# A hybrid mixer block on one core: new order of the products, gate projections between the mixers, VectorE in place of GpSimd

## The chip, the cores and the metric

The kernel runs on one core of a Trainium2 chip. The metric is the device time of one execution in microseconds (us), as the median over repeated executions. A core has five engines that work side by side: TensorE (PE in the profile, with its weight loads as PEld), VectorE (DVE), ScalarE (ACT), GpSimd (POOL) and SyncE (SP, which here only issues transfers). Each engine works through its own list of instructions in order, and waits on semaphores for the others.

## The reference, cut to what matters

One decoder layer on 512 tokens of width 1024, in float32: three token mixers of four heads each beside one another, merged by gates, and then an MLP.

```python
u = rmsnorm(x, g_norm_mix)
proj = u @ w_in                                   # q, k, v, gates of all three mixers
h_m = head_rmsnorm(sigmoid(mo) * mlstm(mq, mk, mv, li, lf), g_hm)
lg  = log_sigmoid(llr @ w_gla_lr + b_gla) / 16
h_l = head_rmsnorm(gla(lq, lk, lv, lg), g_hl) * silu(lr)
qkv = silu(causal_conv([dq, dk, dv], conv_w))     # then l2-normed per head
h_d = head_rmsnorm(gated_deltanet(gq, gk, gv, g_dec, beta), g_hd) * silu(dz)
up  = einsum('bsnc,ncd->bsnd', [h_m, h_l, h_d], w_up)
x   = x + sum_n(sigmoid(gates_n) * up_n) @ w_out
u   = rmsnorm(x, g_norm_mlp)
x   = x + square(relu(u @ w_mlp_in)) @ w_mlp_out
out = rmsnorm(x, g_final)
```

`mlstm`, `gla` and `gated_deltanet` are chunked recurrences along the sequence; the last solves a unit triangular system in each chunk.

## The kernel before, in words

Every large product (projections, up, out, MLP) is done in three passes: each operand is split into a rounded part (`h`) and the rest (`l`), and `mm3` (line 548) issues `al·bh`, `ah·bl`, `ah·bh` into one PSUM bank, 512 columns each. There are 3768 such passes, called wide products below: 96 each for `mv`, `mo`, `dz`, `lv` and `lr`, 24 for `sc`, 48 for each of the 14 projections `dk0` to `lk1` and the 12 gate groups `gt00` to `gt23`, 24 for each of the 12 `up` groups, 192 for `wo`, 768 each for the MLP's `mi` and `mo`. A weight tile of 128 x 1024 is loaded by SP's queue (`load_w`, line 622), rounded by ACT, and its rest is taken by DVE; it feeds 24 wide products. Between them stand small products in plain float32: transposes, and the mixers' 128 x 128 blocks and smaller.

The program is not issued as it is written. `write_block` (line 509) records operations into a graph, and a list scheduler in Python (`Graph.schedule`, line 232, and `run`, line 284) gives each a start time from a table of costs (`cost`, line 192) and emits them in that order on each engine. The wide products are "mains": their order is fixed by the list in `plan` (line 480). All else is placed around them, the operation with the earliest due time first; due times come from a backward pass over the graph. Tiles come from pools of fixed size: `s` has 55 buffers of 516 columns for nearly everything of 128 x 512, `raw`, `wh`, `wl` have three each for weights, `g` and `m` four PSUM banks each. When a pool is empty, an operation that needs a new tile of it stands later in the order.

The order of the mains before is: `mv mo sc`, the six projections of the delta branch (`dk dq dv`), the four of the mLSTM (`mq mk`), `dz`, then gates and up products of the mLSTM branch (`gt00 up00 gt01 up01 ...`), then `lv lq lk` for GLA, gates and up products of the delta branch (`gt20 up20 ...`), `lr`, those of the GLA branch (`gt10 up10 ...`), `wo`, and the MLP. `up0x` needs `hmT`, `up2x` needs `hdT`, `up1x` needs `hlT`, the finished outputs of the mixers.

The parts that the change touches:

- `gen_u` (line 594): eight squares of x on ACT, summed by seven POOL adds into `xacc`, while the first products (`mv`) run on x times the norm's gain.
- `conv_evac` (line 821): three DVE passes per head for the convolution, then a sigmoid on ACT and a product on POOL.
- `gen_scalars` (line 753), `gen_k` (837), `gen_q` (871): masks `em` (eight `s` tiles; two transfers, a POOL add, an exp each), and `ub`, the 32 x 32 diagonal blocks with their sign turned, by 32 small passes, half on POOL.
- `gen_gdn` (line 904): `ub` goes through DRAM into a layout `Z` in which a backward substitution runs as 60 dependent POOL passes (lines 914 to 918); its result `xb` comes back through DRAM, is copied into `em` by 32 small passes, and two levels of block inversion on PE follow, then the loop over four chunks.
- `gen_gla` (line 1134): per head a softplus, cumulative sums (four scans), and for seven block sizes L one or two POOL subtractions into `lw`, an exp on ACT, two DVE products (`lwq`, `lw`), PE products `ll` and copies into `lAT`.
- `merge` (1245), `gen_x2` (1303), `square_of` and `finish` (1398, 1405): more POOL adds and products on 128 x 512 tiles.

Of the kernel before, what the change touches and what calls it, by code (L numbers as in the profile page):

```python
# [12 lines left out]
ALU = mybir.AluOpType  # L13
# [10 lines left out]
SLOTN = 516  # L24
NWARM = 10
NSLOT = 55
# [22 lines left out]
INORDER = ("w", "mq")  # L49
RESERVE = {"s": 6, "m": 1}  # L50

# [54 lines left out]
class Op:  # L106
    __slots__ = ("i", "eng", "calls", "cost", "lat", "preds", "succs", "tiles", "main", "fset", "kind", "start", "fin", "lst", "npred", "ready", "new", "tag", "nbytes", "evac")


class Graph:  # L110
    def __init__(self, nc):
        self.nc = nc
        self.ops = []
        self.main_key = None
        self.open = None
        self.shadow = __import__("concourse.bacc", fromlist=["Bacc"]).Bacc("TRN2", target_bir_lowering=False, num_devices=1)
        self.ntile = 0
        self.gate = []
        self.tensor, self.vector, self.scalar, self.gpsimd, self.sync = (Eng(self, e) for e in ("tensor", "vector", "scalar", "gpsimd", "sync"))

# [30 lines left out]
    def record(self, eng, method, a, k):  # L151
# [7 lines left out]
        if fresh:  # L159
# [3 lines left out]
            op.tag = ""  # L163
            self.ops.append(op)
# [6 lines left out]
        c, lat = self.cost(eng, method, a, k, op)  # L171
# [20 lines left out]
    def cost(self, eng, method, a, k, op):  # L192
# [10 lines left out]
        if eng == "tensor":  # L203
            if method == "transpose":
                return max(0.109, n / 1200), 0.2
            if a[1].t.dt == F32R:
                return max(0.109, n / 2400 + 0.0135), 0.2
            return 2 * max(a[1].shape[-1] / 1200, n / 1200, 0.012) + 0.007, 0.2
        if eng == "scalar":
# [3 lines left out]
            c = 0.09 + n * 0.86e-3  # L213
            if any(isinstance(k.get(x), View) for x in ("bias", "scale")) or (method == "mul" and isinstance(a[2], View)):
                c += 0.08
            if k.get("accum_out") is not None:
                c += 0.11
            return c, 0.12
        if eng == "vector":
            if method in ("tensor_scalar", "tensor_scalar_mul", "tensor_copy", "tensor_scalar_add", "tensor_single_scalar", "memset", "reciprocal") and not ps:  # L220
                return 0.1 + n * (0.55e-3 if method != "reciprocal" else 1.05e-3), 0.1
            if method == "tensor_tensor_scan":
                return 0.12 + n * 2.1e-3, 0.1
            if method == "copy_predicated":
                return 0.1 + n * 1.3e-3, 0.1
            return 0.1 + n * 1.06e-3 + (0.05 if ps else 0), 0.1
        if method in ("memset", "tensor_copy"):
            return 0.15 + n * 0.8e-3, 0.1
        return 0.2 + n * 2.15e-3, 0.1


    def schedule(self, caps, seq, horizon, rounds=2, verbose=False):
# [12 lines left out]
        for r in range(rounds):  # L245
            for o in reversed(ops):
                l = end + 5 - o.cost
                for s in o.succs:
                    l = min(l, s.lst - self.edge(o, s) - o.cost)
                o.evac = o.eng != "tensor" and any(t.whole for t in o.tiles)  # L250
                if o.evac:
                    l = min([l] + [pin[p] + p.cost + EVAC for p in o.preds if p in pin])
                o.lst = min(l, pin[o]) if o in pin else l
            for o in ops:
                if o.evac:
                    o.lst = min(o.lst, max(p.lst + p.cost for p in o.preds) + EVAC)
# [15 lines left out]
        return sorted(ops, key=lambda o: (o.start, o.i))  # L272

# [10 lines left out]
    def run(self, mains, caps, horizon, verbose=False):  # L284
# [10 lines left out]
        waiting = {}  # L295
        for o in ops:
# [8 lines left out]
            if not o.npred and o.main is None:  # L305
                cand[o.eng].append(o)
# [5 lines left out]
        line = {c: [t for o in reversed(ops) for t in o.new if t.cls == c] for c in INORDER}  # L312
        urgent = {c: sorted((o for o in ops if any(t.cls == c for t in o.new)), key=lambda o: -o.lst) for c in RESERVE}
# [25 lines left out]
        while done < total:  # L339
# [4 lines left out]
            for e, fr in free.items():  # L344
# [39 lines left out]
                if bests is None or pick[2] < bests[0]:  # L384
                    bests = pick[2:]
# [15 lines left out]
            for w in waiting.pop(o, ()):  # L401
                w.npred -= 1
                w.ready = max(w.ready, T)
                if w.npred == 0 and w.main is None:
                    cand[w.eng].append(w)
            tight = True
            c = o.cost
# [26 lines left out]
            for s in o.succs:  # L434
# [5 lines left out]
                if s.npred == 0 and s.main is None:  # L440
                    cand[s.eng].append(s)
            if o.main is None:
                cand[o.eng].remove(o)
# [5 lines left out]
    def emit(self, order, pools, phys):  # L449
        nc = self.nc  # L450
        for o in order:
# [15 lines left out]
            for eng, method, a, k in o.calls:  # L467
                f = lambda x: x.real() if isinstance(x, View) else x
                getattr(getattr(nc, eng), method)(*[f(x) for x in a], **{n: f(x) for n, x in k.items()})  # L469
# [10 lines left out]
def plan():  # L480

    merge_of = lambda n: [x for dp in range(4) for x in (f"gt{n}{dp}", f"up{n}{dp}")]
# [1029 lines left out]
```

## Time and profile before

| | |
|---|---|
| median of 3 runs | 1022.69 us (1020.7 to 1024.67) |
| the profiled execution's own time | 1020.38 us |
| its span, first to last instruction | 1018.4 us |
| PE busy | 979.8 us, 96% (4992 products) |
| PEld, DVE, ACT, POOL busy | 809.1, 581.3, 404.7, 201.9 us |
| mean granted TensorE clock | 0.986 |

In the profile nearly every instruction has line L469, where `emit` issues it, so groups are told apart by their tiles. The span is cut into stretches in the second group of rows below. A stretch in which PE has all its time is one in which no mixer holds the products up; the number in brackets behind a busy time is the number of instructions. Because products are pipelined, a PE row lasts longer (0.39 us) than the distance to the next row's start (0.23 us), and a slow stretch can look busy: the distance between starts is the better measure.

### The profile page before, as it was taken

Reading aid. Unit: us, or ns where it says so; the run is one execution under the profiler, and the core shown is the slowest. Engines: PE = TensorE matmul, PEld = TensorE weight load, DVE = VectorE, ACT = ScalarE, POOL = GpSimd, SP = SyncE. Lnnn points to the kernel's source line nnn. Section 1 sums busy time; section 2 is a strip of 40 time slices with the busy share of each in tenths; the row PEclk is TensorE's granted clock in tenths of the full one; section 3 lists DMA queues with packets and bytes.
Section 4 is the critical chain, followed back from the end, with each engine's and each line's share of the span. In section 5 each row is a group of like instructions: output and inputs, shape, how many; then the busy total and the mean of one; then the engine's idle time right before and its main releaser. Section 6 shows DMA issues by size and latency. Waiting matters only on the chain.

```text
span 1018.4 us, 12973 instructions
## 1 busy us (share of the span) xinstructions
PE 979.8 (96%) x4992; PEld 809.1 (79%) x4992; DVE 581.3 (57%) x962; ACT 404.7 (40%) x748; POOL 201.9 (20%) x240
## 2 busy tenths in 40 slices
PE   7999999999996999889999999999999999999996
PEld 5888888787885888777888888888888888888885
DVE  7646634878733365999836454444444544544445
ACT  6342423877221546744324334443223232422412
POOL 4100100309593000867411002200000000100004
PEclk9999999999997999979999999999999999999999
DMA  6233232331423112211341223222333233432302
GB/s 237 83 104 96 90 104 96 102 105 53 113 74 84 63 63 91 63 62 43 104 145 63 91 95 104 83 83 83 107 101 104 73 113 97 138 117 83 104 21 83
DMA packets 37029, 94.65 MB, mean 93 GB/s; under 512 B 7804, under 2 KB 11900, under 8 KB 36968
## 3 DMA queue, kind: packets, MB, share of 16 engines
q1 hardware_dynamic: 36152, 92.51, 28.5%
q10 hardware_dynamic: 720, 1.08, 0.3%
q8 instruction: 39, 0.64, 0.3%
q0 software_dynamic: 96, 0.24, 0.1%
q14 instruction: 22, 0.18, 0.1%
HBM read 91.17 MB, written 2.65 MB: 92 GB/s over the span
## 4 chain that ended last, share of the span: by engine, by line
PE 83%; DVE 10%; issue 3%; ACT 3%; POOL 0%; DMA 0%; DVEq 0%; POOLq 0%; ACTq 0%
PE mop L469 19%; PE mip L469 17%; PE upp L469 5%; PE wop L469 4%; PE mvp L469 3%; PE lvp L469 2%; PE lrp L469 2%; DVE lw L469 1%; PE gt23p L469 1%; PE gt10p L469 1%; PE lk0p L469 1%; PE gt01p L469 1%; PE lq0p L469 1%; PE gt11p L469 1%; PE gt13p L469 1%
## 5 line engine op out<-in xcount | busy, mean ns | idle before, releaser
L469 DVE SCALAR_TENSOR_TENSOR x<-mop,r2c,x 128x512 f32<-128x512 f32 (+1 forms) x65 | 48.1, 740 | 61.0 <-PE mop L469 60.5
L469 POOL TENSOR_SCALAR gf<-gf 128x512 f32<-128x512 f32 x2 | 3.0, 1492 | 225.3 <-DMA gf<-in_g_fin_dram 225.3
L469 POOL TENSOR_TENSOR lw<-lbs 128x260 f32<-128x260 f32 (+12 forms) x52 | 42.6, 846 | 17.3 <-PE ll L469 7.7
L469 POOL TENSOR_TENSOR x<-x,gf 128x512 f32<-128x512 f32 x8 | 10.9, 1357 | 116.1 <-ACT fsq L469 116.1
L469 POOL TENSOR_TENSOR x2acc<-x2acc,x2sq 128x512 f32<-128x512 f32 x7 | 12.6, 1793 | 96.7 <-ACT x2sq L469 96.7
L469 POOL TENSOR_TENSOR cv<-cv,cvs 128x512 f32<-128x512 f32 x12 | 15.4, 1307 | 71.7 <-ACT cvs L469 71.7
L469 PEld LDWEIGHTS ll<-lwq,lw 128*17 128x17 f32 (+3 forms) x320 | 17.9, 133 | 13.2 <-ACT lqe L469 7.0
L469 PE MATMUL ll<-lwq,lw 128*17 128x16 f32 (+3 forms) x320 | 19.3, 217 | 9.0 <-ACT lqe L469 6.6
L469 ACT ACTIVATE lw<-lw 128x512 f32<-128x512 f32 x28 | 17.1, 628 | 23.3 <-POOL lw L469 22.3
L469 ACT ACT_TABLE_LOAD x19 | 24.4, 1283 | 1.0 <-PEq L1500 0.7
L469 DVE SCALAR_TENSOR_TENSOR sg<-sg,upp 128x512 f32<-128x512 f32 x24 | 17.1, 713 | 10.0 <-PE upp L469 9.8
L469 DVE TENSOR_TENSOR al<-rl,ah 128x512 fp32r<-128x512 f32 x32 | 22.1, 690 | 1.0
L469 POOL TENSOR_TENSOR lge<-lge,lgw 128x512 f32<-128x512 f32 x4 | 5.7, 1440 | 84.7 <-ACT lgln L469 84.7
L469 DVE TENSOR_TENSOR rl<-rl 128x512 f32<-128x512 f32 x32 | 22.1, 692 | 0.0
L469 ACT ACTIVATE ah<-rl 128x512 fp32r<-128x512 f32 x32 | 20.3, 633 | 1.2
L469 DVE TENSOR_TENSOR lw<-lw,lks 128x260 f32<-128x260 f32 (+6 forms) x28 | 20.6, 752 | 0.3
L469 ACT ACTIVATE rl<-mip 128x512 f32<-128x512 f32 x32 | 18.9, 591 | 1.7 <-PE mip L469 1.7
L469 POOL TENSOR_TENSOR tmU<-Z 64x30 f32<-64x30 f32 (+14 forms) x30 | 17.1, 569 | 12.5 <-DMA Z<-scr_u 10.2
L469 POOL TENSOR_TENSOR Z<-Z,tmU 64x30 f32<-64x30 f32 (+14 forms) x30 | 19.1, 636 | 2.3
L469 DVE TENSOR_TENSOR x2T<-xr,wop 128x512 f32<-128x512 f32 x8 | 5.5, 688 | 22.1 <-PE wop L469 22.1
L469 POOL TENSOR_TENSOR sce<-sce,scw 128x512 f32<-128x512 f32 x1 | 1.3, 1299 | 74.4 <-ACT scln L469 74.4
L469 DVE TENSOR_TENSOR lwq<-lw,lqs 128x256 f32<-128x256 f32 x24 | 15.3, 651 | 0.2
(1586 smaller groups left out, 3312.7 us busy)
## 6 DMA issues: line engine op xcount, KB each, us to landing
xk<-in_xT_dram SPq DMA_DIRECT2D x8, 256.0 KB, 5.4
em<-scr_rows SPq DMA_DIRECT2D x16, 128.0 KB, 4.5
xr<-in_xT_dram SPq DMA_DIRECT2D x8, 256.0 KB, 3.9
nm<-scr_rows SPq DMA_DIRECT2D x4, 256.0 KB, 3.6
out_dram<-x SPq DMA_DIRECT2D x4, 256.0 KB, 2.1
out_dram<-x ACTq DMA_DIRECT2D x4, 256.0 KB, 2.0
mo00r<-in_w_tm_dram SPq DMA_DIRECT2D x1, 512.0 KB
mo01r<-in_w_tm_dram SPq DMA_DIRECT2D x1, 512.0 KB, 6.7
```

The costliest lines, as they stand in the source:

```text
L469: getattr(getattr(nc, eng), method)(*[f(x) for x in a], **{n: f(x) for n, x in k.items()})
```

## The change

The mains get a new order, in which the gate groups stand between the projections and the up products of the three branches are mixed:

```
mv mo dk0 mq1 sc mk0 dq1 dq0 mk1 mq0 dk1 gt01 dv0 gt00 dv1 gt02 lq0 gt03 gt20
up00 up02 lk0 lq1 lv lk1 up03 dz up01 gt22 gt13 up20 gt12 gt21 up21 lr gt23 up22
up23 gt10 up10 up12 gt11 up11 up13 wo mi0, then mi/mo of the MLP as before
```

The due times now come from a backward pass (`due`) that lets DVE and ACT do one thing at a time. Some costs are set anew and raised by a margin (DVE 1.1, ACT 1.05). An engine `either` is added: copies and scalings are placed by the scheduler on ACT or, where ACT is not free within 1.5 us, on DVE. Weight tiles are handed out in the order of the mains. All arithmetic of POOL goes to DVE (or to `either`); POOL keeps memsets and two transfers. `em` becomes one tile of its own (`eall`), so that 32 small passes for `ub` become 4, the 32 copies of `xb` 4, the 16 of `pZ` 2 and the 8 of `pZ2` 2. `mv` becomes four tiles of its own. The pool `s` goes from 55 buffers of 516 columns to 44 of 512. The convolution's sigmoid becomes a tanh, with the factor 2 taken out later. The scale by -1/16 in GLA moves into the exps, and its four scans per head become one.

```diff
-NSLOT = 55
+NSLOT = 44
+LEAVE = 1.5
+MARGIN = {"vector": 1.1, "scalar": 1.05}
...
+            if e in free:
+                c = o.alts["scalar"] if o.alts else o.cost
+                o.lst = free[e] = min(-l, free[e] - c)
...
+                    if o.alts and e == "vector" and max(free["scalar"], o.ready) < T + LEAVE:
+                        continue
...
             if k:
-                nc.gpsimd.tensor_add(acc, acc, sq)
+                nc.vector.tensor_add(acc, acc, sq)
...
-        v = slot(f"mv{t}", n=516).rearrange("p (h d) -> p h d", h=4)
+        v = one(f"mv{t}", [P, 516]).rearrange("p (h d) -> p h d", h=4)
...
+    eall = one("em", [P, 4, 4, 2, P])
+    em = [[eall[:, h, 2 * u:2 * u + 2] for u in range(2)] for h in range(4)]
...
-            nc.scalar.activation(sg, a, AF.Sigmoid)
-            nc.gpsimd.tensor_mul(a, a, sg)
+            nc.scalar.activation(sg, a, AF.Tanh, scale=0.5)
+            nc.vector.scalar_tensor_tensor(a, sg, 1.0, a, op0=ALU.add, op1=ALU.mult)
...
-            nc.gpsimd.tensor_mul(t_, Z[:, 0:s, s:s + 1].broadcast_to([64, s, n]), Z[:, s:s + 1, s + 1:].broadcast_to([64, s, n]))
-            nc.gpsimd.tensor_add(Z[:, 0:s, s + 1:], Z[:, 0:s, s + 1:], t_)
+            nc.vector.tensor_mul(t_, Z[:, 0:s, s:s + 1].broadcast_to([64, s, n]), Z[:, s:s + 1, s + 1:].broadcast_to([64, s, n]))
+            nc.vector.tensor_add(Z[:, 0:s, s + 1:], Z[:, 0:s, s + 1:], t_)
...
-        for h in range(4):
-            for i in range(4):
-                for u in range(2):
-                    (nc.vector if u else nc.gpsimd).tensor_copy(em[h][u][blk(i, 32), :, 1, blk(i, 32)], xb4[blk(i, 32), 2 * u:2 * u + 2, h, :])
+        for i in range(4):
+            nc.either.copy(eall[blk(i, 32), :, :, 1, blk(i, 32)], xb4[blk(i, 32)].rearrange("p c h t -> p h c t"))
...
-        for c in range(4):
-            nc.vector.tensor_tensor_scan(b[:, blk(c)], ones.broadcast_to([P, P]), yb[:, blk(c)], 0.0, op0=ALU.mult, op1=ALU.add)
+        nc.vector.tensor_tensor_scan(b, cone, yb, 0.0, op0=ALU.mult, op1=ALU.add)
...
-            nc.gpsimd.tensor_sub(w3[:, :, :L + 1], b3[:, :, L:L + 1].broadcast_to([P, nb, L + 1]), b3[:, :, :L + 1])
+            nc.vector.tensor_sub(w3[:, :, :L + 1], b3[:, :, L:L + 1].broadcast_to([P, nb, L + 1]), b3[:, :, :L + 1])
...
-        nc.gpsimd.tensor_mul(x2[t][1], x2[t][1], gf[1])
+        nc.vector.tensor_mul(x2[t][1], x2[t][1], gf[1])
```

## Rows read from the trace of the kernel before

**Rows 1.** The page's first part: busy time of each engine.

```profile
PE 979.8 (96%) x4992; PEld 809.1 (79%) x4992; DVE 581.3 (57%) x962; ACT 404.7 (40%) x748; POOL 201.9 (20%) x240
```

**Rows 2.** Windows by stretch: length; busy of PE, PEld, DVE, ACT, POOL; clock; DMA.

```profile
7.42:25.00 17.58, 17.58 (x63) 13.86 (x64) 17.31 (x18) 13.44 (x23) 10.48 (x10) 1.00 0.68 256
25.00:175.00 150.00, 150.00 (x678) 124.31 (x678) 82.70 (x110) 54.07 (x70) 8.04 (x9) 1.00 0.30 95
175.00:250.00 75.00, 70.81 (x403) 58.35 (x402) 61.69 (x176) 59.32 (x185) 30.03 (x32) 0.98 0.30 92
250.00:300.00 50.00, 50.00 (x228) 41.11 (x227) 29.29 (x45) 13.07 (x17) 36.55 (x53) 1.00 0.33 95
300.00:350.00 50.00, 40.34 (x382) 34.05 (x381) 18.73 (x55) 14.29 (x47) 13.50 (x38) 0.90 0.23 64
350.00:425.00 75.00, 75.00 (x383) 63.49 (x382) 49.01 (x110) 45.97 (x85) 16.32 (x14) 1.00 0.23 74
425.00:500.00 75.00, 65.84 (x561) 54.08 (x560) 72.60 (x132) 33.19 (x62) 54.09 (x61) 0.93 0.21 68
500.00:700.00 200.00, 200.00 (x943) 166.02 (x942) 96.55 (x125) 75.05 (x129) 18.13 (x11) 1.00 0.29 95
```

**Rows 3.** Timeline of PE: starts of wide products, and of two sets of small ones.

```profile
426.99 0.39 PE L469 MATMUL gt21p<-xh,gt210l 128*128 128x512 f32 x1
427.22 0.39 PE L469 MATMUL gt21p<-xl,gt210h 128*128 128x512 f32 x1
...
340.01 1.05 PE L469 MATMUL pu<-vn,kn 128*128 128x128 f32 x8
340.90 1.06 PE L469 MATMUL po<-vn,em 128*128 128x128 f32 x8
```

**Rows 4.** Waits of PE: for whom, us in total, times, longest.

```profile
PE pY L469 <- issue: 9.7, 1, 9.7
...
PE ll L469 <- ACT lqe L469: 6.6, 1, 6.6
```

**Rows 5.** Timeline of POOL around the substitution, its first and last passes.

```profile
245.82 5.06 POOL L469 TENSOR_SCALAR ub<-em 32x64 f32<-32x64 f32 x12
...
270.17 0.25 POOL L469 TENSOR_TENSOR tmU<-Z 64x30 f32<-64x30 f32 x1 [10.19 <-DMA Z<-scr_u]
...
310.73 0.23 POOL L469 TENSOR_TENSOR Z<-Z,tmU 64x30 f32<-64x30 f32 x1
```

**Rows 6.** Waits of DVE: for whom, us in total, times, longest.

```profile
DVE em L469 <- DMA xb<-scr_x: 11.1, 1, 11.1
```

**Rows 7.** Critical chain, one piece: first transposes of the delta branch's output.

```profile
382.70 1.31 PE hdo L469 x12
```

**Rows 8.** Lines by form: POOL and DVE passes, busy, mean ns, idle before.

```profile
L469 POOL TENSOR_TENSOR sg<-sg,sg 128x512 f32<-128x512 f32 x8 | 11.4, 1424 | 18.6 <-DVE sg L469 18.6
L469 DVE TENSOR_TENSOR sg<-sg,sg 128x512 f32<-128x512 f32 x8 | 5.5, 692 | 0.3
L469 DVE TENSOR_TENSOR me<-me,mqk 128x256 f32<-128x256 f32 x4 | 1.7, 418 | 0.8 <-PE mqk L469 0.5 <-ACT me L469 0.3
L469 DVE TENSOR_TENSOR rs_t<-rs_i 128x16 f32<-128x16 f32 x9 | 1.6, 175 | 0.3
L469 DVE TENSOR_TENSOR gt200l<-gt200r,gt200h 128x1024 fp32r<-128x1024 f32 x1 | 1.2, 1226 | 3.5 <-ACT gt200h L469 3.5
```

**Rows 9.** Timeline of DVE in the head, beside POOL passes and without.

```profile
19.03 1.78 DVE L469 TENSOR_TENSOR mv4l<-mv4r,mv4h 128x512 fp32r<-128x512 f32 x1
...
21.40 0.68 DVE L469 TENSOR_TENSOR mv5l<-mv5r,mv5h 128x512 fp32r<-128x512 f32 x1
```

**Rows 10.** Timeline of the tail.

```profile
1010.87 1.10 DVE L469 TENSOR_SCALAR x<-x,fy,fh 128x512 f32<-128x512 f32 x1
...
1013.10 1.26 POOL L469 TENSOR_TENSOR x<-x,gf 128x512 f32<-128x512 f32 x1 [1.42 <-ACT fsq L469]
...
1014.25 1.00 DVE L469 TENSOR_SCALAR x<-x,fy,fh 128x512 f32<-128x512 f32 x2
```

More of the change, by code (lines that the diff above doesn't have):

```diff
@@ L106 @@
 class Op:
-    __slots__ = ("i", "eng", "calls", "cost", "lat", "preds", "succs", "tiles", "main", "fset", "kind", "start", "fin", "lst", "npred", "ready", "new", "tag", "nbytes", "evac")
+    __slots__ = ("i", "eng", "calls", "cost", "lat", "preds", "succs", "tiles", "main", "fset", "kind", "start", "fin", "lst", "npred", "ready", "new", "tag", "nbytes", "evac", "alts")
 class Graph:
@@ L170, in record @@
         op.calls.append((eng, method, a, k))
-        c, lat = self.cost(eng, method, a, k, op)
+        if eng == "either":
+            op.alts = {e: self.cost(e, WORDS[e][method], a, k, op)[0] * MARGIN.get(e, 1.0) for e in WORDS}
+            c, lat = min(op.alts.values()), 0.12
+        else:
+            c, lat = self.cost(eng, method, a, k, op)
+            c *= MARGIN.get(eng, 1.0)
         op.cost += c
@@ L245, in schedule @@
         for r in range(rounds):
[L246 to L256, printed above, removed]
+            self.due(pin, end)
             span = self.run(mains, caps, horizon, verbose)
@@ L272, in schedule, with due, offer @@
         return sorted(ops, key=lambda o: (o.start, o.i))
+    def due(self, pin, end):
+        import heapq
+        heap, free, left = [], {"vector": end + 5, "scalar": end + 5}, {}
+        def offer(o):
+            l = end + 5 - o.cost
+            for s in o.succs:
+                l = min(l, s.lst - self.edge(o, s) - o.cost)
+            o.evac = o.eng != "tensor" and any(t.whole for t in o.tiles)
+            if o in pin:
+                l = min(l, pin[o])
+            elif o.evac:
+                l = min([l] + [pin[p] + p.cost + EVAC for p in o.preds if p in pin])
+            heapq.heappush(heap, (-l, -o.i, o))
+        for o in self.ops:
+            left[o] = len(o.succs)
+        for o in self.ops:
+            if not left[o]:
+                offer(o)
+        while heap:
+            l, _, o = heapq.heappop(heap)
+            e = "scalar" if o.alts else o.eng
+            o.lst = -l
+            if e in free:
+                c = o.alts["scalar"] if o.alts else o.cost
+                o.lst = free[e] = min(-l, free[e] - c)
+            for p in o.preds:
+                left[p] -= 1
+                if not left[p]:
+                    offer(p)
+        for o in self.ops:
+            if o.evac:
+                o.lst = min([o.lst] + [max(pin.get(p, p.lst) + p.cost for p in o.preds) + EVAC])
     def edge(self, p, o):
@@ L295, in run, with offer @@
         waiting = {}
+        def offer(o):
+            for e in o.alts or (o.eng,):
+                cand[e].append(o)
+        for o in ops:
+            if o.alts:
+                o.eng = None
         for o in ops:
@@ L480, in plan @@
 def plan():
-    merge_of = lambda n: [x for dp in range(4) for x in (f"gt{n}{dp}", f"up{n}{dp}")]
-    seq = (["mv", "mo", "sc", "dk0", "dq0", "dv0", "dk1", "dq1", "dv1", "mq0", "mk0", "mq1", "mk1", "dz"] + merge_of(0)
-           + ["lv", "lq0", "lk0", "lq1", "lk1"] + merge_of(2) + ["lr"] + merge_of(1) + ["wo", "mi0"])
+    seq = """mv mo dk0 mq1 sc mk0 dq1 dq0 mk1 mq0 dk1 gt01 dv0 gt00 dv1 gt02 lq0 gt03 gt20 up00 up02 lk0 lq1 lv lk1 up03 dz up01
+    gt22 gt13 up20 gt12 gt21 up21 lr gt23 up22 up23 gt10 up10 up12 gt11 up11 up13 wo mi0""".split()
     for g in range(1, 8):
@@ L750, in write_block @@
     scr = nc.dram("scr_rows", (12, S))
-    em = [[None, None] for _ in range(4)]
+    eall = one("em", [P, 4, 4, 2, P])
+    em = [[eall[:, h, 2 * u:2 * u + 2] for u in range(2)] for h in range(4)]
     def gen_scalars():
@@ L975, in gen_gdn @@
             z4 = pZ[0:64].rearrange("p (c h t) -> p c h t", c=2, h=4)
-            for h in range(4):
-                nc.scalar.copy(em[h][half][0:64, :, 1, 64:128], z4[:, :, h])
+            nc.either.copy(eall[0:64, :, 2 * half:2 * half + 2, 1, 64:128], z4.rearrange("p c h t -> p h c t"))
         Sst = None
@@ L1000, in gen_gdn @@
             vn = slot(f"vn{c}")
-            nc.scalar.copy(vn, pn)
+            nc.either.copy(vn, pn)
             if c < 3:
@@ L1020, in gen_gdn @@
             else:
-                nc.scalar.copy(o_, po)
+                nc.either.copy(o_, po)
             ss = small("sso", 4)
@@ L1277, in lv_evac @@
         lv[t] = slot(f"lv{t}")
-        nc.scalar.copy(lv[t], ps)
+        nc.either.copy(lv[t], ps)
     def lr_evac(t, ps):
```

158 lines of the change are left out of this document (85 added, 73 removed).

## The prediction

> **What bounds the kernel now.** First the page's busy times: PE has 96% of the span, DVE 57%, POOL 20% [rows 1]. PE is the engine to look at, and the question is where its other time is. Second, the windows by stretch [rows 2]. In 25:175, 250:300, 350:425 and 500:700 PE is busy all the time; in 175:250, 300:350 and 425:500 it is not, and there the clock was granted at 0.98, 0.90 and 0.93 of the full 2.4 GHz as well. Third, the distances between starts of PE rows. A wide product follows the last after 0.227 us in a full stretch (426.99 to 427.22), a 128 x 128 product after 0.111 us (eight between 340.01 and 340.90) [rows 3]. I take each form's median distance as its price, count the starts in each stretch, and call what is left the loss (first and last of the 4992 starts: 7.42 and 1009.99 us):
>
> - 425:500: 163 wide x 0.227 = 37.0, 396 small ones 20.8; 75 - 57.8 = 17.2, by the single distances 17.1 us lost
> - 300:350: 108 wide = 24.5, 272 small 13.0; 50 - 37.5 = 12.5 (12.4) us lost
> - 175:250: 161 wide = 36.5, 240 small 27.2; 75 - 63.7 = 11.3 (11.2) us lost
> - 7.42:25: 63 wide = 14.3; 17.6 - 14.3 = 3.3 us lost
> - the full stretches lose 0.4 to 0.5 us each, 500:700 2.0, the MLP behind 700 some 3.5.
>
> So 40.7 us are lost in three places, all where a mixer's chain runs and too few products are left that don't need it. The idle time that the windows show in these is less, 4.2 + 9.7 + 9.2 = 23.1 us, because a slowed product looks long rather than late.
>
> Fourth, what PE waits for. The 9.7 us before `pY` [rows 4] lie behind the substitution: `ub` is done at 250.9, the POOL loop runs from 270.17 to 310.96, DVE then waits for `xb` (11.1 us) [rows 5, 6], and the branch's output reaches PE at 382.70 [rows 7], 132 us after `ub`. The `ll` wait of 6.6 us [rows 4] lies in 425:500, where DVE is busy 72.6 of 75 us and POOL 54.1 [rows 2]: DVE is the bound there. And a DVE pass beside a POOL pass is slow: `mv4l` took 1.78 us, `mv5l` 0.68 us once POOL's adds were over [rows 9]; over the whole trace the 230 passes that lie beside POOL passes take some 64 us more than the same forms alone (these two are an example of each kind).
>
> The Trainium skill (Perfetto Trace Analysis, section Identifying the Most-Contended Engine) says to judge TensorE by the share of LDWEIGHTS and not by matmul busy time. Read literally that is 79% [rows 1], so 21% or 209 us of room, against my 50. The trace disagrees: with nothing in the way (25:175) PEld has 124.3 of 150 us, 83% [rows 2], so 83% is full, and 809.1 / 0.829 = 976 us would remain, 42 us below the span.
>
> **The change part by part.** The products are the same, so PE's own work (951 us at these prices) stays; only losses can go, or come.
>
> *New order.* In 175:250 the mLSTM had only `dz` and `gt00` between its last projection and `up00`: 96 + 48 wide products, 33 us. Now between `mq0` and `up00` stand nine groups of 48: 98 us. The delta branch had `merge` of the mLSTM, `lv`, `lq`, `lk` as cover; now from `dv1` to `up20` stand 9 x 48 + 2 x 96 + 4 x 24 = 720 wide products, 163 us, against a chain of 132 us behind `ub` [rows 5, 7]. GLA had only the delta branch's merge, 288 products or 65 us, while its DVE work filled 75; now between `lk1` and `up10` stand 2 x 96 + 6 x 48 + 6 x 24 = 624, 142 us, and heads 0 and 1 can begin before `lq1`. I take the waits of all three stretches as gone, up to what the new order leaves: the mixed stretches that are covered now lose 0.5 in 75 and 2.0 in 200 us, so some 3 us over 350 us of mixing. I add 4 us for places where an order written ahead doesn't meet the chip, as at `pY`. 40.7 - 7 = 33.7 us gained. Bounds: 23 (only the idle that the windows show) and 40.7; a loss, below nothing, is the third rival's.
>
> *POOL's arithmetic on DVE.* The same 128 x 512 form costs 1.424 us on POOL and 0.692 on DVE [rows 8]. Of POOL's 201.9 us some 186 are arithmetic that goes to DVE: x 0.486 = +90 us. Off DVE go the 64 us of passes slowed by POOL, and some 15 us of small passes that merge or go to ACT. DVE ends at 581 + 90 - 64 - 15 = about 592 us, as much as before, with POOL's 202 gone. In 25:700 the same sum gives 411 + 86 - 50 - 15 = 432 of 640 us, 67%: no bound on average. This costs nothing while the new order spreads it; if it did not, 425:500 is the price: 17 us.
>
> *The substitution on DVE.* 60 passes of 30 to 240 elements, 9920 in all. No DVE row has this form; 128 x 16 took 0.175 and 128 x 256 0.418 us [rows 8], so about 0.16 + 0.0010 per element: 9.6 + 10 = 20 us, against 40.8 on POOL. Bounds: 20 without anything between, and 20 + 60 x 0.69 = 61 if a 128 x 512 pass stood before each. I take 30: the chain is 10 us shorter. It is covered, so it counts only in the rivals.
>
> *The head.* PE takes 12 wide products per block of x, 2.7 us; DVE needs two passes, 1.8 + 1.7 beside POOL's adds [rows 9], 3.5 us: DVE sets the pace there. Now it needs three of 0.7, 2.1 us. Of the 3.3 us lost I take 2.5 (0 to 3.3).
>
> *The tail.* The last products of x with the gain leave POOL (1.26 us, begun at 1013.10, done just after the last DVE scaling at 1014.25 began), and the scaling at 1010.87 took 1.10 beside it, where two take 1.00 at the end [rows 10]. Gain 0.5 us, from -0.7 (one more 0.69 pass in line) to 1.1.
>
> *Fewer passes, tanh for sigmoid, one scan, `either`.* These shorten DVE and ACT, which are covered; 0, with -1 to 2 as bounds. The pool `s` is a rival below.
>
> Sum: 33.7 + 2.5 + 0.5 = 36.7, rounded down to 36 us. The profiled execution took 1020.38 us, 2.0 over its span of 1018.4; it becomes 984. The median of the runs stands 2.3 above the profiled one: 1022.7 - 36 = **987 us**.
>
> **The rivals.**
>
> *DVE binds in part.* From `lk0` to `gt10` DVE has GLA, the delta branch's substitution and chunk loop (30 + 10), a 1.23 us split for each 24 of some 820 products (42) [rows 8], and merges (30). GLA is an estimate: per head 28 passes of 128 to 512 columns for the seven block sizes at 0.45 on average, and 12 of 0.69 for the softplus, scan and `lAT`, 21 us, x 4 = 84. That is 196 of some 235 us (820 x 0.227 and 50 of small products), 83%. With in-order queues at that load a late pass holds up products. Half of the 40.7 stays: 1022.7 - 20 - 3 = 1000 us. For it: DVE at 97% was the bound in 425:500. Against: 350:425 has DVE at 65% and loses nothing.
>
> *The stalls only move.* The chains are as long as they were, and the pool gives new waits that eat the gain: 1022.7 within 5 us. For it: the order is again fixed ahead. Against: cover of 98, 163 and 142 us where it was 33, 100 and 65.
>
> *Slower: the pool `s` runs dry at `lk1`.* When `em` and `mv` had died, 55 buffers were free for the rest; now it is 44. At `lk1` the order holds ten gate tiles, eight halves of `hmT`, eight of `lq` and `lk`, four of `lv` and three that stay: 33. The delta branch needs 16 (`knT`, `kn`, `bv`, `qc`) until its chunk loop ends, and only 11 are left. So PE stands at `lk1` until that loop is done. From `dv1` to the end of `lk1` lie 7 x 48 + 2 x 24 + 96 = 480 products, 109 us, and I put small ones at 30 us (27 lay in 175:250, 13 in 300:350); the chain is some 15 us of `gen_k` to `gen_q` (an estimate: 20 passes of 0.69), then 132 less 10: 137 of 139. It just fits with 30 us for the substitution. If each of its 60 passes, and 20 of the block inversions and the chunk loop, waits behind one 128 x 512 pass (0.692 us [rows 8]), the chain grows by 55 us and PE stands 53: 1022.7 - 36 + 53 = 1040 us. It makes the kernel slower from 38 us of delay on. Against: the scheduler counts buffers and DVE's queue when it places passes.
>
> *More than the three places.* All 40.7, the head and 4 us of the rest: 975 us. The rule of the Trainium skill above, read literally, would go lower still; by the 83% of rows 2 it can't.
>
> **How the numbers follow.** Most stalls gone (976 to 996): 0.65. DVE binds in part (996 to 1012): 0.19. More than the three places (under 976): 0.03. Stalls only move (1012 to 1028): 0.04. Pool runs dry, slower: 0.09. A measurement of this kernel tells about 0.5%, 5 us, from no change, so faster means under 1017.6 and slower over 1027.8: faster 0.65 + 0.19 + 0.03 + 0.01 = 0.88, same 0.03, slower 0.09. The range 975 to 1008 leaves out the lower tail, part of the partly bound case, and the last two: about 2 in 10.
>
> **What would show it.** In the profile after: POOL near 10 us; DVE near 590 with no 128 x 512 pass over 0.8 us; PE busy in every window from 25 us to the MLP's end, clock 1.00 in each; no wait of PE above 2 us behind the first product; `hdo`, `ll` and `mn` without idle before them; the substitution's 60 passes in 20 to 35 us. Wrong: a wait of PE for `lk1`, `lv` or `lq1` with ACT waiting on a buffer (pool), or windows with DVE above 23 of 25 us and PE under 24 (DVE bound), or a PE share that stays at 96%.

## The result, and the profile after

The changed kernel takes 976.0 us (median of 4 runs, 975.25 to 976.91), the kernel before 1022.34 beside it; the ratio is 0.955 (95% interval 0.952 to 0.957). The prediction was 987 (975 to 1008). The profiled execution took 976.91 us, its span is 975.1, 43.3 us less than before. The busy line, and the windows by stretch with the columns of [rows 2]:

```profile
PE 964.2 (99%) x4992; PEld 804.0 (82%) x4992; DVE 580.9 (60%) x1065; ACT 408.5 (42%) x764; POOL 5.4 (1%) x20
```

```profile
6.54:25.00 18.46, 18.24 (x72) 14.67 (x73) 14.90 (x24) 12.48 (x22) 0.00 (x0) 0.91 0.75 280
25.00:150.00 125.00, 125.00 (x595) 103.92 (x594) 86.59 (x162) 65.51 (x142) 0.53 (x1) 1.00 0.37 112
150.00:200.00 50.00, 50.00 (x280) 41.78 (x279) 38.56 (x121) 27.23 (x83) 0.67 (x3) 1.00 0.23 71
200.00:375.00 175.00, 175.00 (x1045) 147.33 (x1044) 106.67 (x250) 83.59 (x154) 0.64 (x2) 1.00 0.27 86
375.00:500.00 125.00, 125.00 (x850) 103.90 (x849) 86.66 (x166) 56.42 (x115) 1.92 (x4) 1.00 0.24 77
500.00:600.00 100.00, 100.00 (x497) 84.23 (x497) 60.77 (x95) 41.74 (x80) 0.00 (x0) 1.00 0.33 106
```

PE is busy in all of them but for 0.2 us at the first product, and from 25 us on the clock is 1.00, where 175:250, 300:350 and 425:500 had gaps and 0.98, 0.90, 0.93 [rows 2]. In these windows DVE is nowhere above 77%. PE's waits (columns as in [rows 4]) are three, all in the first 8 us; `pY` and `ll` are gone:

```profile
PE mvp L525 <- ACT mv0h L525: 1.5, 1, 1.5
PE pss L525 <- DVE onem L525: 1.1, 1, 1.1
PE mvp L525 <- DVE ones L525: 0.2, 1, 0.2
```

Groups of DVE passes (count, busy us, mean ns of one). A 128 x 512 product costs 688 ns, as it did alone before [rows 8]. The 60 passes of the substitution are busy for 19.2 us, which is the 20 that I worked out:

```profile
L525 DVE TENSOR_TENSOR sg<-sg,sg 128x512 f32<-128x512 f32 x16 | 10.8, 688 | 0.2
L525 DVE TENSOR_TENSOR lw<-lbs 128x260 f32<-128x260 f32 (+12 forms) x52 | 21.0, 448 | 7.9 <-PE ll L525 7.8
L525 DVE TENSOR_TENSOR tmU<-Z 64x30 f32<-64x30 f32 (+14 forms) x30 | 9.6, 319 | 0.1
L525 DVE TENSOR_TENSOR Z<-Z,tmU 64x30 f32<-64x30 f32 (+14 forms) x30 | 9.6, 319 | 0.1
```

But DVE's timeline shows them from 197.1 to 250.9 us, 54 us, since other passes stand between them; three rows of its beginning and the last:

```profile
197.09 0.19 DVE L525 TENSOR_TENSOR tmU<-Z 64x30 f32<-64x30 f32 x1
197.21 0.14 DVE L525 SCALAR_TENSOR_TENSOR d<-d 128x2 f32<-128x2 f32 x1
197.32 0.20 DVE L525 TENSOR_TENSOR Z<-Z,tmU 64x30 f32<-64x30 f32 x1
...
250.67 0.18 DVE L525 TENSOR_TENSOR Z<-Z,tmU 64x30 f32<-64x30 f32 x1
```

**Where the 43.3 us came from.** I take the distance from each PE start to the next, less one price for its form (the changed kernel's median: 227 ns for a wide product, 111 for 128 x 128), and sort what is over. Up to 25 us it is the head, with the time ahead of the first product. Behind that, where one wide product follows another by less than 12 ns too much, it is "per product"; all else is "stalls". Tail: last start to the end.

| us | head | stalls | per product | tail |
|---|---|---|---|---|
| before | 10.8 | 40.5 | 7.2 | 8.4 |
| after | 6.6 | 8.0 | 0.7 | 8.4 |
| gained | 4.2 | 32.5 | 6.5 | 0.0 |
| predicted | 2.5 | 33.7 | 0 (-1 to 2) | 0.5 |

The stalls came out as forecast. Whether for the reason given, the six runs that follow ask; two questions more are where "per product" comes from and what the head's gain is.

### The profile page after: what moved, and what is told of

It reads as the page before. It is cut to its first block, busy times and chain, and to the rows that moved or that the text cites. A ratio compares the mean times of both kernels' runs of the same rounds, so it can differ in the third digit from the quotient of the medians.

```text
span 975.1 us, 12773 instructions
## 1 busy us (share of the span) xinstructions
PE 964.2 (99%) x4992; PEld 804.0 (82%) x4992; DVE 580.9 (60%) x1065; ACT 408.5 (42%) x764; POOL 5.4 (1%) x20
## 4 chain that ended last, share of the span: by engine, by line
PE 98%; DVE 0%; DMA 0%; ACT 0%; issue 0%; DVEq 0%; POOLq 0%
PE mop L525 20%; PE mip L525 18%; PE upp L525 7%; PE wop L525 4%; PE mvp L525 2%; PE lrp L525 2%; PE dzp L525 2%; PE lvp L525 2%; PE ll L525 2%; PE gt22p L525 1%; PE gt13p L525 1%; PE gt20p L525 1%; PE gt12p L525 1%; PE gt21p L525 1%; PE dq0p L525 1%; PE dv0p L525 1%
## 5 line engine op out<-in xcount | busy, mean ns | idle before, releaser
L525 DVE TENSOR_TENSOR lw<-lbs 128x260 f32<-128x260 f32 (+12 forms) x52 | 21.0, 448 | 7.9 <-PE ll L525 7.8
L525 DVE TENSOR_TENSOR lw<-lw,lks 128x260 f32<-128x260 f32 (+6 forms) x28 | 13.1, 498 | 0.0
L525 ACT COPY lAT<-ll 17x64 f32<-17x64 f32 (+3 forms) x32 | 7.2, 231 | 11.4 <-PE ll L525 11.0
L525 DVE COPY_PREDICATED lAT<-cs,ll 128x256 f32<-128x256 uint8 x16 | 9.3, 578 | 4.0 <-PE ll L525 4.0
L525 ACT ACTIVATE fsq<-x 128x512 f32<-128x512 f32 (+1 forms) x9 | 5.3, 585 | 14.1 <-DVE x L525 14.1
L525 DVE TENSOR_TENSOR me<-me,mqk 128x512 f32<-128x512 f32 (+3 forms) x16 | 7.5, 485 | 6.2 <-PE mqk L525 5.9
L525 DVE TENSOR_TENSOR sg<-sg,sg 128x512 f32<-128x512 f32 x16 | 10.8, 688 | 0.2
L525 ACT ACTIVATE cvs<-cv 128x512 f32<-128x512 f32 x12 | 7.5, 628 | 7.4 <-DVE cv L525 7.4
L525 PEld LDWEIGHTS mn<-mv,me 128*128 128x128 f32 x80 | 10.1, 191 | 0.5
L525 PE MATMUL mqk<-mqs,mks 128*128 128x512 f32 (+3 forms) x32 | 10.4, 432 | 0.0
```

## Experiments: which part takes the stalls away

The theory of the prediction: the new sequence puts enough products beside each mixer's chain. The rival: the shorter chains (POOL's arithmetic gone, fewer passes, other due times) would have needed no new sequence. The new sequence alone can't be measured: in the kernel before, with or without the new due times, and in the changed kernel with the old due times or 43 buffers, the plan runs out of room for its tiles.

**The old sequence in the changed kernel.**

```diff
-    seq = """mv mo dk0 mq1 sc mk0 dq1 dq0 mk1 mq0 dk1 gt01 dv0 gt00 ...
+    merge_of = lambda n: [x for dp in range(4) for x in (f"gt{n}{dp}", f"up{n}{dp}")]
+    seq = (["mv", "mo", "sc", "dk0", "dq0", "dv0", ... "mk1", "dz"] + merge_of(0)
+           + ["lv", "lq0", "lk0", "lq1", "lk1"] + merge_of(2) + ["lr"] + merge_of(1) + ["wo", "mi0"])
```

> The changed kernel with the products in the sequence of the kernel before; engines, passes, due times and pool stay the changed ones. T1 (the sequence gives the cover): the losses of the mixers come back, in the same three places (in front of the branches' up products), about 34 us: over 1000 us, PE's share at 96 to 97%. T2 (the work taken off POOL and the fewer passes shorten the chains enough): the old cover suffices now, at most 985 us. Half and half would be about 993.

1000.86 us (1000.62 to 1001.36). The total is what the theory asked for, but not the places. PE's waits:

```profile
PE mvp L525 <- ACT mv0h L525: 9.3, 1, 9.3
PE pkt L525 <- DVE kn L525: 5.3, 1, 5.3
```

The head alone lost 11.1 us more. ACT's timeline shows why: the squares of x stand ahead of the first weights there, and `mv0h` is made at 13.6 instead of 5.9 us. The stalls grew only from 8.0 to 20.6, and none is left in front of `pY`. So without the new sequence the mixers lose 12.6 us, not 33. The expectation was met by an accident elsewhere, and the theory holds for about a third of its sum.

**POOL's arithmetic put back, new sequence kept.** Every product and sum that the change took off POOL, but for the subtractions into `lw`:

```diff
-                nc.vector.tensor_add(acc, acc, sq)
+                nc.gpsimd.tensor_add(acc, acc, sq)
...
-            nc.vector.tensor_mul(t_, Z[:, 0:s, s:s + 1]...
+            nc.gpsimd.tensor_mul(t_, Z[:, 0:s, s:s + 1]...
```

> The changed kernel, its new sequence kept, with the arithmetic put back on POOL wherever it stood there before, the substitution's 60 passes too; only GLA's subtractions into lw stay on DVE. T1 (the sequence): the mixers' chains get longer and DVE passes beside POOL's are slow again (some 45 to 60 us of DVE time over the trace), but all of it lies beside the filler: 974 to 985 us, the head's 2 us included. T2 (the engines): PE stands again in front of the up products, above 990 us.

983.15 us (982.43 to 983.81). POOL is busy 141.9 us again, and DVE passes beside its passes cost 37 us more than the same forms alone (64 before, 0 after). Yet the stalls are 10.4: the new sequence covers that. Of the 7 us lost 4.0 are the head, where the warm-up products stand behind the first wide ones again (from 25.6 us; see the last experiments) and `pr`, a load that the first products wait for, landed 1.0 us later; so little of it is the price of POOL's passes. The Trainium skill (SBUF — State Buffer, section Who interferes with whom) says that a DVE instruction with two SBUF inputs contends with a GpSimd one that reads SBUF. The 64, 37 and 0 us agree in the main: of the 64, some 40 lie in passes with two tensor inputs, the other 23 in passes with one (scalings and copies). What it costs the kernel is another matter: 2.4 us of stalls here.

**Old sequence and old due times.** In the plan, `self.due(...)` is replaced by the loop of the kernel before:

```diff
-            self.due(pin, end)
+            for o in reversed(ops):
+                l = end + 5 - o.cost
+                for s in o.succs:
+                    l = min(l, s.lst - self.edge(o, s) - o.cost)
+                ...
```

> The changed kernel with the sequence of the products AND the due times of the kernel before; engines, fewer passes and the pool stay the changed ones. The run with the old sequence and the new due times lost 11 us in its head alone (the squares of x were put ahead of the first weights) and 22 us in the mixers, against 9 in the changed kernel and 44 before. If the engines do it and the due times nothing: the head as in the changed kernel, the mixers again some 22 us: 988 to 990 us. If the due times carried part of the gain: the mixers 30 to 44 us, 997 to 1010.

1007.69 us (1006.79 to 1008.58), stalls 36.5: the second case. The due times, which I had not priced at all, are worth 16 us of stalls under the old sequence.

**Old sequence, arithmetic of the mixers back on POOL, new due times.** The sequence as in the first run, and the edit of the second without the sum of squares and the scaling of `mv`, but with `lw`.

> The changed kernel with the old sequence of the products and with the arithmetic of the mixers, merges and the tail back on POOL, GLA's subtractions into lw too (only the sum of squares of x and the scaling of mv stay on DVE); due times, the merged passes and the pool stay the changed ones. If either cover is enough by itself and both were lacking before: the mixers lose 40 us or more, about 1008 to 1015. If the fewer passes and the due times did a good part: the mixers lose 20 to 30, 988 to 998.

989.31 us (988.4 to 989.81): the second case again by its time, with stalls of 16.6, below the 20 to 30 that it named. With the old sequence and POOL at work, most of the gain is there already, and it is faster than the first run, which has the same sequence and DVE alone (8 of the 12 us between them are the first run's head).

**Sequence, engines and due times as before.** The last kernel with the old due times.

> The changed kernel with sequence, due times and engines of the mixers' arithmetic as before: what is left of the change is the merged passes, the copies that go to ACT or DVE, costs, weight order and the pool of 44 buffers of 512 columns. Theory (due times and sequence do it): the mixers lose 36 to 42 us as before, only the 6 to 7 us of the operands' places and 1 of the head are gained: 1012 to 1016. Rival (these small edits carry the gain that the due times were credited with): under 1000.

1001.86 us (1001.16 to 1002.64), where the theory said 1012 to 1016 and the rival under 1000: a miss for the theory, and nearly the rival's case. Of the 21 us gained 7.3 are per product (-0.1 left); the stalls fell by 10.9, to 29.6. So the merged passes, the copies that go to ACT or DVE, `em`'s own tile and the new costs carry a third of the stalls. The gain is GLA's: around 425:500, where 17 us were lost, some 7 are. Of the other two places one only moved into the other: the gap at 300:350 is gone, and between 175 and 250 us some 10 us more are lost than before, with the substitution where it was. PE's longest waits:

```profile
PE mvp L535 <- ACT mv0h L535: 7.8, 1, 7.8
PE mqk L535 <- DVE me L535: 4.5, 2, 3.9
PE hmo L535 <- DVE hmhl L535: 3.7, 1, 3.7
PE ll L535 <- DVE lw L535: 2.0, 1, 2.0
```

What the due times do is seen in one pair, this kernel and the one above, which differ by them alone. The transfers of the delta branch's masks (`em`) and the substitution's first half, as views of one tile (shortest, median and longest in ns; first and last start in us). With the old due times:

```profile
L535 SPq DMA_DIRECT2D em<-scr_rows x16: 359/467/480, 207.5 to 216.6; - x16
L535 POOL TENSOR_TENSOR tmU<-Z x30: 227/544/1503, 269.8 to 310.6; 64x30 f32<-64x30 f32 x2, 64x58 f32<-64x58 f32 x2, 64x84 f32<-64x84 f32 x2, 64x108 f32<-64x108 f32 x2
```

With the new ones:

```profile
L525 SPq DMA_DIRECT2D em<-scr_rows x16: 359/458/1597, 135.0 to 144.3; - x16
L525 POOL TENSOR_TENSOR tmU<-Z x30: 231/529/1486, 199.0 to 239.7; 64x30 f32<-64x30 f32 x2, 64x58 f32<-64x58 f32 x2, 64x84 f32<-64x84 f32 x2, 64x108 f32<-64x108 f32 x2
```

The substitution is as long in both, 41 us on POOL, but it begins 71 us sooner. What the two rules do stands in the code: the old one dates a pass back from what needs it, as if it had its engine to itself; the new one lets DVE and ACT do one thing at a time, so work that piles up ahead of a date gets dates further ahead. In the kernel before, `ub` itself was late: DVE's half of its passes (the view of that tile) ended at 261 us, 131 us after the delta branch's last projection:

```profile
L469 DVE TENSOR_SCALAR ub<-em x16: 176/600/1237, 249.7 to 260.9; 32x64 f32<-32x64 f32 x16
```

**The new due times alone, in the kernel before.**

```diff
+    def due(self, pin, end):
+        ...
-            for o in reversed(ops): ...
+            self.due(pin, end)
```

> The kernel BEFORE with one thing changed: the due times come from the backward pass that lets DVE and ACT do one thing at a time. Old sequence, POOL's arithmetic, 55 buffers, all passes and costs as before. Theory (the due times start the delta branch's chain earlier: its substitution began at 270 us with the old ones and at 199 with the new ones, same sequence and same engine): the wait of 9.7 us in front of pY goes, the substitution starts near 200 us, the mixers lose 17 to 22 us instead of 40: 999 to 1003 us. Rival (the due times help only together with the raised costs, the merged passes and em's tile of its own): no more than 8 us, 1014 to 1022.

1008.61 us (1008.08 to 1009.1), ratio 0.987 (0.985 to 0.989): between the cases. The 9.7 us in front of `pY` are gone; the masks' first transfer is issued at 178.6 instead of 217.1 us, and the substitution starts 45 us sooner than before [rows 5]:

```profile
L494 SPq DMA_DIRECT2D em<-scr_rows x16: 359/438/472, 178.6 to 187.5; - x16
L494 POOL TENSOR_TENSOR tmU<-Z x30: 230/550/1502, 225.5 to 266.8; 64x30 f32<-64x30 f32 x2, 64x58 f32<-64x58 f32 x2, 64x84 f32<-64x84 f32 x2, 64x108 f32<-64x108 f32 x2
```

But the stalls fell to 28.0, not to about 20: GLA's waits for `lw` stay (6.0 us in six); there, from 375 to 475 us, DVE is still busy 91% of the time. So the theory's mechanism is right and its price of 18 to 23 us was too high for this kernel: 12.5.

**The six side by side,** with the kernels before and after. "Passes" means the merged passes, copies, `em`'s tile, costs and the new pool. In the two rows with "POOL" alone beside new passes DVE keeps the sums of squares and the scaling of `mv`. The head goes mostly with the 20 warm-up products: they stand ahead of the first wide product in the sixth and the last row (in the sixth the squares then delay the weights), and behind 25 us in all others.

| sequence | due times | arithmetic | passes | time | stalls | head |
|---|---|---|---|---|---|---|
| old | old | POOL | old | 1022.3 | 40.5 | 10.8 |
| old | new | POOL | old | 1008.6 | 28.0 | 9.8 |
| old | old | POOL | new | 1001.9 | 29.6 | 9.8 |
| old | old | DVE | new | 1007.7 | 36.5 | 9.4 |
| old | new | POOL | new | 989.3 | 16.6 | 9.5 |
| old | new | DVE | new | 1000.9 | 20.6 | 17.7 |
| new | new | POOL but `lw` | new | 983.2 | 10.4 | 10.6 |
| new | new | DVE | new | 976.0 | 8.0 | 6.6 |

From the first row to the last by the third, fifth and seventh, the stalls fall by 10.9 (passes), 13.0 (due times), 6.2 (sequence, with `lw`) and 2.4 (the rest of the arithmetic); together 32.5. The order in which one takes them matters: the sequence is worth 6 us of stalls beside POOL's arithmetic and 12.6 without it, and taking the arithmetic off POOL costs 6 and 12 us of time under the old sequence (of the 12, 8 are that head) and gains 7 under the new (4 of them the head).

## Experiments: the operands' places

Behind 700 us both kernels do the same products without a wait, and there the wide ones that have an operand in pool `s` (`mo`, `up`, `wo`) stood 232 ns apart before and 227 after, those without (`mi`) 227 in both. The pool's buffers were 2080 bytes (516 columns) and are 2048. In the changed kernel, by the addresses of the build, both operands of every wide product lie at the same place modulo 512 bytes. So a room was left behind pool `s`, which moves the pools behind it against it and changes nothing else:

```diff
         phys[k] = (ctx.enter_context(tc.tile_pool(name=f"p_{k}", bufs=n, **kw)), k, shape, {})
+        if k == "s":
+            ctx.enter_context(tc.tile_pool(name="p_pad", bufs=1)).tile([P, 8], F32, name="pad")
```

> The changed kernel with 32 bytes left free between pool s and the pools behind it: the same instructions in the same order, but the two operands of a product that has one of them in pool s no longer lie at the same place modulo 512 bytes. T3 (the relative place of the two operands costs some 5 ns a wide product, which the kernel before paid): mo, up and wo products go from 227 to about 232 ns apart, some 1440 of them, +5 to +7 us, 981 to 983 us; the MLP's first products (mi) stay at 227. Rival (what the kernel before paid came from other work beside the products): 976 us, within 1 us.

983.99 us (983.22 to 984.87). 8 us more than the changed kernel, for 32 bytes. Products with one operand in `s` stand 233 ns apart on average, those with none 227 as before; `mi`, both of whose operands moved by the 32 bytes together, is among these, so it is the place of one against the other and not the move. PE's timeline (start in us, duration, tile): five distances from 800.21 to 801.38, 234 ns each.

```profile
800.21 0.39 PE L525 MATMUL mop<-mo301h,al 128*128 128x512 f32 x1
800.44 0.40 PE L525 MATMUL mop<-mo301l,ah 128*128 128x512 f32 x1
...
801.38 0.40 PE L525 MATMUL mop<-mo301h,ah 128*128 128x512 f32 x1
```

> As the run with 32 bytes left free behind pool s, but with 512: the same instructions in the same order, other addresses, and the operands of a product lie again at the same place modulo 512 bytes. Theory (the relative place modulo 512 bytes is what costs): 976 us, within 1 us of the changed kernel, wide products 227 ns apart. Rival (any shift, or the room left free, costs): 982 to 984.

975.77 us (975.43 to 977.04). Five distances from 800.03 to 801.16, 226 ns each:

```profile
800.03 0.39 PE L525 MATMUL mop<-mo300h,al 128*128 128x512 f32 x1
800.26 0.39 PE L525 MATMUL mop<-mo300l,ah 128*128 128x512 f32 x1
...
801.16 0.39 PE L525 MATMUL mop<-mo301h,ah 128*128 128x512 f32 x1
```

> As the runs with 32 and 512 bytes left free behind pool s, with 256. If the places of the operands count modulo 512 bytes: 981 to 984 us as with 32. If they count modulo 256 or less: 976, as with 512.

976.7 us (975.23 to 977.0); `mo` at 226.7 ns. So the effect is there, and 512 is not its measure: 256 bytes cost nothing, 32 bytes cost 6 ns a product. What lies between wasn't tried. The kernel before isn't explained product by product: there those with one operand in `s` stood 229 to 233 ns apart at every place, and the 102 whose two operands lay at the same place modulo 512 bytes 232 like the rest. So a product's own two operands don't decide it there; whether its neighbours in the stream do is open. That its 7 us go with the buffers is shown by the runs as a whole: per product 7.2 and 7.7 us in the two kernels with 516 columns, and -0.3 to 1.0 in all with 512 and no room, or room of 256 or 512 bytes.

The Trainium skill (SBUF — State Buffer, section Who interferes with whom) gives PE two read ports that don't depend on each other, one for the moving operand and one for weight loads, and says that PE never waits on anyone. These runs disagree in so far as the place of one operand against the other moves the distance from 226.7 to 233 ns with the same instructions in the same order; the measurement decides, and where in PE the 6 ns go they don't show.

## Experiments: the head

In the kernel before, the 20 small products of `onem` that warm PE up came at 27.2 us, behind the first 72 wide products. In the changed kernel they run while the loads are under way (timeline):

```profile
1.05 3.98 PE L525 MATMUL pss<-onem 128*128 128x128 f32 x20 [1.05 <-DVE onem L525]
...
6.54 0.51 PE L525 MATMUL mvp<-mv0h,vl 128*128 128x512 f32 x1 [1.51 <-ACT mv0h L525]
...
8.04 0.63 PE L525 MATMUL mvp<-mv0h,vl 128*128 128x512 f32 x1
...
8.47 0.63 PE L525 MATMUL mvp<-mv0l,vh 128*128 128x512 f32 x1
```

Then PE stood 1.5 us, and the wide products came 0.43 us apart until 10.6 us. The clock there was granted at 0.50, its lower level (1.2 GHz), by the window 7.6:11 (columns as in [rows 2]):

```profile
7.60:11.00 3.40, 3.40 (x9) 2.63 (x8) 3.40 (x7) 3.40 (x8) 0.00 (x0) 0.50 1.04 395
```

The kernel before did the same for longer. Its wide products stand 0.43 us apart from 8.74 to 13.44 us, and 0.23 behind that, with POOL's adds still under way beside DVE [rows 9]:

```profile
8.74 0.63 PE L469 MATMUL mvp<-mv0h,vh 128*128 128x512 f32 x1
9.17 0.63 PE L469 MATMUL mvp<-mv0h,vl 128*128 128x512 f32 x1
...
13.44 0.48 PE L469 MATMUL mvp<-mv1l,vh 128*128 128x512 f32 x1
13.75 0.39 PE L469 MATMUL mvp<-mv1h,vh 128*128 128x512 f32 x1
```

Its windows show 1.00 up to there, but its trace has no record of the clock ahead of a rise at 13.6 us; from the distances I take it as at the lower level too. Three kernels differ in the length of the warm-up alone (`NWARM = 10`, two small products each, replaced by 18, 15 and 0).

> The changed kernel with 18 warm-up products instead of 10, so that PE does not stand between them and its first product. Theory: the first ten or so wide products stand 0.2 us further apart because the clock is granted at its lower level until 10.6 us, after an idle stretch of 1.5 us; without that stretch the clock is full by then and 1.5 to 2 us go: about 974 us. Rival: the arrival of the weights and of DVE's split sets the head's pace, and the clock only lies beside it: 976 us, within 0.5; or the longer warm-up delays the first product, up to +1 us.

975.74 us (975.4 to 976.33): 0.3 less in the median, 1.1 in the span. The ten slow products are gone, but the first one starts at 7.38 instead of 6.54, behind the warm-up.

> 15 warm-up products. With 18 the clock was full from the first weight load on and the ten slow products (2 us) were gone, but the warm-up ended 0.8 us after the first weights were there, so 1.1 us of span were left as gain. With 15 the warm-up should end at about 6.6 us, where the weights come: about 974 us, 1.5 to 2 us under the changed kernel. Rival: the clock falls back in a short gap behind the warm-up, or DVE's first splits (the second product waits for mv0l until 7.2 us) set the pace: 975.5 to 976.

975.31 us (975.25 to 975.4). The head is 3.8 us instead of 6.6. The two windows 5:10 and 10:15 (columns as above), of the changed kernel, of the run with 512 bytes, and of this one:

```profile
5.00:10.00 5.00, 3.27 (x9) 2.38 (x9) 4.23 (x8) 5.00 (x10) 0.00 (x0) 0.76 0.96 363
10.00:15.00 5.00, 5.00 (x21) 4.00 (x21) 5.00 (x9) 5.00 (x10) 0.00 (x0) 0.90 1.05 393
```

```profile
5.00:10.00 5.00, 3.71 (x16) 2.69 (x15) 4.03 (x8) 4.97 (x10) 0.00 (x0) 1.00 0.97 326
10.00:15.00 5.00, 5.00 (x24) 4.14 (x23) 5.00 (x9) 5.00 (x10) 0.00 (x0) 1.00 1.05 397
```

```profile
5.00:10.00 5.00, 5.00 (x27) 4.28 (x26) 4.25 (x8) 5.00 (x10) 0.00 (x0) 1.00 0.97 370
10.00:15.00 5.00, 5.00 (x24) 4.14 (x23) 5.00 (x9) 5.00 (x10) 0.00 (x0) 1.00 1.06 395
```

The first two have the same instructions. In the one profile the clock was granted at 0.76 and 0.90 behind 1.5 us of idle, in the other at its full 2.4 GHz behind 1.1 us. So the slow products come in some executions of the changed kernel only (the one profiled with 256 bytes has them too, at 0.75, and took 976.86 us; the one with 512 took 975.5). That fits the spread of its runs, 975.2 to 977.0 over it and the two neutral paddings, but only the profiled ones show their clock. The longer warm-up leaves 975.25 to 975.4. In the median that is 0.07% less: the fastest version tried, and no difference that a measurement can tell.

> The changed kernel without its ten warm-up products. In the kernel before they came behind the first products, in the changed kernel they run from 1 to 5 us, before the weights come. Theory (the head's gain is mostly the clock that the warm-up brings up, not DVE's shorter passes): the first ten or so wide products stand 0.43 us apart, the head loses 9.4 us instead of 5 to 6.6: 979 to 980.5 us. Rival (loads and DVE's passes set the head): 976, within 0.7.

977.31 us (976.67 to 978.9), below the 979 that I asked for. The products are 0.43 to 0.73 us apart at first, as expected, and the span is 2.0 us longer. The head's loss is 4.2 greater, but the 20 small products, 20 x 0.111 = 2.2 us, are missing from the work, and I had not taken them off. The rest isn't the clock's alone: the first product started at 7.93 instead of 6.54, since a load (`pr`) landed 1.4 us later in that execution. So of the 4.2 us that the change gained in the head, 2.2 are the warm-up's own time, moved to where PE has nothing to do, and 0.9 the first product's earlier start (7.42 to 6.54 us), as much as `pr` landed sooner in the profiled execution (3.4 us after its issue, 4.3 before), which the change doesn't explain. Some 0.9 more is the clock: up to the end of the slow stretch the products lose 3.1 us in the kernel before and 2.2 in the changed one. About 0.2 is left for DVE's shorter passes. Where the clock is full from the first product on, the run with 15 gains 1.6 us of span more.

## Why the prediction was right in its sum, and where it was wrong

- **What bounds the kernel**: right. PE's products set the time, the losses lay in three places, 951 us of product time stayed.
- **Mixers, 33.7 predicted, 32.5 measured; cause in part wrong.** The step that failed is "New order": it compared cover with chain, 33 with the wait, 163 with 132, 142 with 75 us, and gave the whole sum to the sequence. The cover was counted from different places: the new 163 us run from `dv1` to `up20`, and by the same count the old sequence had 912 products there (`mq`, `mk`, `dz`, the mLSTM's merge, `lv`, `lq`, `lk`, `gt20`), 207 us, more than the new one; for GLA it had 432 from `lk1` to `up10`, 98 us and not 65. What failed before was the start: `dv1` was done at 130 us, and `ub` only at 261 (the 250.9 of the prediction is POOL's half of its passes). In the changed kernel `ub` is done at 189 us, before `dv1`. The prediction took the chains' starts as given [rows 5 to 7] and priced the due times nowhere; and it put the "fewer passes" at 0 "because they are covered", although 425:500, with DVE at 97%, was the place where they are not. With the old sequence these two take 23.9 of 40.5 us. Each of the three parts overlaps the others, so each looks sufficient when it is the only one worked out. That the sum came out is luck in part: it was right because the parts that it priced at nothing were in the change too. The 7 us left as residue: 8.0.
- **POOL's arithmetic on DVE, at nothing**: right under the new sequence (2.4 us of stalls gained; the 4 us of the head are mostly the warm-up's place and `pr`), wrong under the old one, where it costs 6 to 12. DVE was 581 us, as forecast to 2%, with the 64 us of slowed passes gone.
- **The substitution, 30 us**: wrong, 54. The passes cost 19.2 as worked out; one other pass stands before 52 of them, which the prediction had only in its upper bound. It was covered, as said, so it cost nothing.
- **The head, 2.5**: 4.2, and for other reasons. The step that failed put it on DVE's pace beside POOL's adds. PE's rows show the clock instead, and from 13.75 us on no loss to speak of: of the 4.2, 2.2 are the place of the warm-up, 0.9 the load of `pr`, 0.9 the clock, and at most 0.2 DVE's passes.
- **The tail, 0.5**: 0.0 (8.43 and 8.40). The products with the gain are off POOL, but the last three scalings still stand in line (1.45 us for three).
- **"Others 0, -1 to 2"**: 6.5, the largest miss of the sum. It goes with the column count of the pool's buffers, which the diff shows and I read as room only. Without it the time would have been about 976.0 + 6.5 = 982.5 us.
- **The 11 us between 987 and 976.0**: 6.6 are the terms above (43.3 instead of 36.7), 1 is rounding, and 3.4 come from the step from spans to medians, since the profiled execution before was 2 us faster than its median and the one after 0.9 slower. So 976.0 lies only 1 us inside the range.
- **The rivals.** DVE as the bound: no, at most 77% in the windows above, and never the 23 us in 25 that the prediction named (21.4 at most). Pool `s` running dry at `lk1`: no wait there; but the room is tight, since with 43 buffers the plan runs out. "More than the three places": it came to that in the total, by a term that was in no case.
- **The signs named**: POOL 5.4, DVE 581, PE full from 25 us, no wait over 2 us: as said. Of the 128 x 512 passes, which were to stay under 0.8 us, one took 0.81 and the four scans 1.21. Substitution in 20 to 35 us: failed.

## What to carry to other kernels

When a change has several parts that attack one stall, work out what each does with the others absent, the planner's dates among them; the first that suffices on paper takes all the credit. A stall is ended as well by starting the chain sooner as by more work beside it, so ask of each chain not only how long it is but what set its first instruction's time. And look at the addresses when buffer sizes change: with PE at 99% of the span, the 6 ns that 32 bytes cost on each of 1344 wide products (`mo`, `up`, `wo`) are 8 us.

## What the runs showed of the hardware that was not expected

- The place of a product's two operands against each other: 226.7 ns a wide product (0, 256 and 512 bytes of shift), 233 with 32 bytes. In the kernel before, with buffers of 2080 bytes, 232 ns at nearly every place.
- The same instruction stream had the clock granted at 0.76 from 5 to 10 us in one execution and at 1.00 in another, where PE idled 1.5 and 1.1 us between the warm-up and the first product.
- The vector `pr` (41 KB, first in POOL's queue) landed 3.2 to 3.8 us after its issue in nine of the profiles and 4.0 to 4.8 in five, the kernel before and the one without a warm-up among them, which moves the whole head by as much. What decides that was not found.
